# Preparing attention outputs one head earlier, and taking three quarters of the first merge products of four blocks into the last two heads

## The chip, the cores and the metric

One core of a Trainium2 chip runs one program: one layer of a hybrid bidirectional encoder. The metric is device time in microseconds (us) of that program; a change is measured against the kernel before on the same chip. On this core, TensorE (PE) multiplies matrices into PSUM, VectorE (DVE), ScalarE (ACT) and GpSimd (POOL) work elementwise, and SyncE (SP) issues most DMA transfers. Each engine takes its instructions in a fixed order.

## The reference, cut to what matters

The part of the layer that matters here is latent attention (MLA) with 16 heads over a prompt group of 256 tokens and a sample group of 1024 tokens, and what follows it:

```
s = (q_nope · k_nope + q_rope · k_rope) * scale
p = softmax(s);  o_a[head] = p @ v_a[head]                  # 16 heads of 64 columns
merged = sigmoid(gate_a) * (o_a @ p_a) + sigmoid(gate_b) * (o_b @ p_b)
x = x + gate * (merged @ w_out)
```

`o_b` is the output of the dilated attention; its half of `merged` has been computed earlier and lies in DRAM.

## The kernel before, in words

Tokens are 1280 columns in three chunks `CH`: two of 512 (sample) and one of 256 (prompt). Every float32 operand of a product is split into a high and a low part (`H`/`L`), so that each product of the reference is three matmuls: high by high, high by low, low by high.

**Heads** (loop at L1348 to L1365). A head has 17 steps: for two chunks eight key tiles each, then one step for the prompt group. A step computes scores (`scores`, L1172 to L1174, three matmuls into a PSUM tile `S`, three buffers), `soft` (L1126 and L1127 on ACT: the exponential twice, into `p` and `ph`; then `pl = p - ph` on POOL, L81, or on DVE for a chunk's first tile and the prompt), and a running sum of `p` on DVE (`ac`). The products with the values (`values`, L1210 and L1211) come three steps later (`LAG`). Beside each step, `fill` (L1334) advances two things: `tops`, which computes the row maxima of the head that comes next (`row_max`: a matmul L1107 into a PSUM tile `mi`, two buffers, and a DVE reduce L1108), and a side generator chosen by `others(h)` (L1313): projections of later heads, `row_sums` (L1147 to L1159: sums of `p` by PE, then through DRAM, reciprocals to `rz_d`). The side generator's pace is a number from `RATE` per step, against the cost that it yields. At the end of an even head, and of head 15, the rest of the side generator is run.

**Outputs.** Each pair of heads leaves its unnormalised output in DRAM (`oa_d`). `prep(k)` (L1251 to L1264) loads pair k's output and two halves of its reciprocals (three DMAs), multiplies them on DVE (`or<-or,or`), casts the high part on ACT (`x<-or`, L1263) and takes the low part on POOL (`x<-or,x`). In head 14 the side generator does this for pairs 0 to 5 in chunk 0, and then `row_sums(6)`; in head 15 it loads and splits weight block 0 of `p_a` (`pa_some`), prepares pair 6, and loads blocks 1 to 3. Pair 7 stays in SBUF and is prepared after the last head, behind the zb sums (L1372) that give its reciprocals. Heads 12 and 13 have no such work: head 13 has nothing in its side generator.

**Merge.** `merge(ms, c)` (L1420 to L1440) computes, for output blocks m of 128 columns, eight pairs by three matmuls into a PSUM tile `pe`; the first call takes blocks 0 to 3 of chunk 0 together: pairs 0 to 6 of each block, then pair 7 of each. Then, per block: `ga` and `mb` are loaded (256 KB each) into tiles `gm`, a sigmoid on ACT, `ga = ps * ga` on DVE, `ga += mb` on POOL, a cast to the high part on ACT (`R<-gm`, L1439), the low part on DVE. The `gm` tiles are a ring of four buffers. Blocks 4 to 7 follow one at a time (L1469 to L1476); ahead of each, `prep_r1` (L1452) prepares two pairs for chunks 1 and 2 together (tiles `R`, one load of 384 KB and two of 96 KB), and weight blocks 6, 7 and 0 are loaded. After that a loop (L1492 to L1497) goes over the eight blocks again for chunks 1 and 2, with weights loaded anew, and a `w_out` load for each.

The order of instructions on an engine is set when the program is built, by priorities and modelled times; all `mk` rings of buffers make a load wait until an earlier tile has been read for the last time.

Of the kernel before, what the change touches and what calls it, by code (L numbers as in the profile page):

```python
# [46 lines left out]
def kernel(  # L47
# [11 lines left out]
    def mk(pool, shape, dt=F32, tag=None, bufs=None):  # L59
        count[0] += 1  # L60
        kw = {}
        if bufs is not None:
            kw["bufs"] = bufs
        return pool.tile(shape, dt, name=f"{tag or 't'}_{count[0]}", tag=tag or f"u{count[0]}", **kw)

    def open_pool(name, side=None, space=None):
        kw = dict(space=space) if space is not None else dict(side=side)
        cm = tc.tile_pool(name=name, bufs=1, reuse_waits="tile", **kw)
        return cm, cm.__enter__()

    def close_pool(cm):
        cm[0].__exit__(None, None, None)
# [4 lines left out]
    def dve_tt(out, a, b, op):  # L77
        nc.vector.tensor_tensor(out=out, in0=a, in1=b, op=op)  # L78
# [50 lines left out]
    v_d = dram.tile([KD, P, NT, 2, 2, 64], F32R, name="v_d")  # L129
    m_d = dram.tile([NH, T], F32R, name="m_d")  # L130
    qr_d = dram.tile([2, 4 * P, T], F32R, name="qr_d")
    oa_d = dram.tile([KD, P, T], F32, name="oa_d")
    z_d = dram.tile([KD, 2, T], F32, name="z_d")
    rz_d = dram.tile([KD, 2, T], F32, name="rz_d")
# [892 lines left out]
    psM = open_pool("psM", space=PSUM)  # L1027
    okeep = {}
    LEAD = 5
    RATE = (3600, 700, 960, 960)  # L1030
    PB, LAG = (4, 5, 5), 3

    def mi():
# [235 lines left out]
    def x0(c=0):  # L1269
        return mk(opl, [P, 512], F32R, tag="x0", bufs=2 * KD)  # L1270

    def prep_some(ks):
        for k in ks:
            prep(k, (0,), or_tile, x0)
            yield 1000

    pa_w = {}

# [7 lines left out]

    oaH, oaL = [[None] * KD for _ in CH], [[None] * KD for _ in CH]
    def tail_pools():
        nonlocal opl, ocm, eacm
        close_pool(lcm)  # L1290
        close_pool(kcm)
        ocm = open_pool("oa", "right")
        opl = ocm[1]
        eacm = open_pool("ea", "right")
        okeep["o"] = mk(opl, [P, T], tag="o7", bufs=1)
        yield 0

    ocm = opl = eacm = None
# [11 lines left out]
    def projections(p_):  # L1310
        yield from ahead([job_p(p_, "k"), job_p(p_, "q")])

    def others(h):  # L1313
        p_ = h // 2
        if h == 0:
            return projections(1)
        if h % 2 == 0 and h < NH - 2:
            return chain(side[0], row_sums(p_ - 1))
        if h % 2 and p_ + 2 < KD:
            return projections(p_ + 2)  # L1320
        if h == NH - 2:
            return chain(tail_pools(), prep_some(range(KD - 2)), row_sums(p_ - 1))
        if h == NH - 1:
            return chain(pa_some((0,)), prep_some((KD - 2,)), pa_some((1, 2, 3)))
        return chain()

    def chain(*gens):
        for g in gens:
            yield from g
# [18 lines left out]
    for h in range(NH):  # L1348
        while h not in ready:
            next(tops)  # L1350
        now[0] = h
        while later:
            later.pop(0)()
        side = [others(h), 0.0, 0.0, (h > 0) + max(0, h - NH + 3)]
        hd = Head(h)
        for c, kt in [(c, kt) for c in range(2) for kt in range(NS)] + [(2, 0)]:
            pend.append((hd, c, kt, hd.step(c, kt)))
            fill()
            if (c, kt) == (0, LAG + 1) and h + 1 < NH:
                value_load(h + 1)  # L1360
            if len(pend) > LAG:
                p_ = pend.pop(0)
                p_[0].values(*p_[1:])
        if h % 2 == 0 or h == NH - 1:
            run(side[0])  # L1365
    for p_ in pend:
        p_[0].values(*p_[1:])
# [40 lines left out]
    epl = ecm[1]  # L1408
    psE = open_pool("psE", space=PSUM)

    def mm3_part(ps, w, x, ks, first, last):
        (wh, wl), (xh, xl) = w, x
        for k in ks:
            nc.tensor.matmul(ps, lhsT=wh[k], rhs=xh[k], start=first and k == ks[0], stop=False)
            nc.tensor.matmul(ps, lhsT=wh[k], rhs=xl[k], start=False, stop=False)
            nc.tensor.matmul(ps, lhsT=wl[k], rhs=xh[k], start=False, stop=last and k == ks[-1])

    mgH, mgL = [[chunk_set(0)] for _ in range(2)]

    def merge(ms_, c):  # L1420
        c0, n = CH[c]
        cs_ = slice(c0, c0 + n)
        pss = [mk(psE[1], [P, 512], tag="pe", bufs=8)[:, 0:n] for _ in ms_]
        x = (oaH[c], oaL[c])
        if len(ms_) > 1:
            for m, ps in zip(ms_, pss):
                mm3_part(ps, pa_w[m], x, range(KD - 1), True, False)
            for m, ps in zip(ms_, pss):
                mm3_part(ps, pa_w[m], x, range(KD - 1, KD), False, True)
        else:  # L1430
            mm3_part(pss[0], pa_w[ms_[0]], x, range(KD), True, True)
        for m, ps in zip(ms_, pss):
            ga, mb = [mk(epl, [P, 512], tag="gm", bufs=4)[:, 0:n] for _ in range(2)]
            nc.sync.dma_start(out=ga, in_=ga_d[m, :, cs_])
            nc.sync.dma_start(out=mb, in_=mb_d[m, :, cs_])
            nc.scalar.activation(out=ga, in_=ga, func=AF.Sigmoid)
            dve_tt(ga, ps, ga, ALU.mult)
            pool_tt(ga, ga, mb, ALU.add)
            nc.scalar.copy(out=mgH[c][m], in_=ga)  # L1439
            sub_dve(mgL[c][m], ga, mgH[c][m])  # L1440
# [530 lines left out]
```

## Time and profile before

| what | value |
|---|---|
| runs of the kernel before, us | 2473.57, 2468.44, 2470.86 (median 2470.86) |
| the profiled execution, us | 2468.41 |
| its span, us | 2466.6 (1.8 less than its time) |
| PE busy, share of the span | 95% |
| DVE, ACT, POOL busy | 61%, 44%, 45% |

All times in the trace are from the start of the span. In the page, PE's busy share dips below nine tenths in few slices; the stretch of this change is from 1260 to 1483 us. A PE that shows busy is not always at full speed: the granted clock (PEclk, 1.00 is 2.4 GHz, 0.50 is 1.2 GHz) falls after pauses.

### The profile page before, as it was taken

How to read it: one execution, taken by the hardware profiler on the slowest of the kernel's cores; microseconds unless marked ns; L12 is line 12 of the kernel's file. 1: busy time of each engine (PE TensorE's matmuls, PEld its weight loads, DVE VectorE, ACT ScalarE, POOL GpSimd, SP SyncE). 2: the span in 40 equal slices, each digit the busy share in tenths (PEclk: the TensorE clock that was granted, in tenths of full speed). 3: DMA queues.
4: the chain of work that ended last, by engine and by line, in shares of the span. 5: the costliest groups of instructions: out<-in, count | busy, mean ns of one | idle time of the engine just before them, and what ended most of it. 6: DMA issues, size and time to landing. Idle time of an engine off the chain costs nothing.

```text
span 2466.6 us, 36993 instructions
## 1 busy us (share of the span) xinstructions
PE 2355.0 (95%) x13177; PEld 1994.2 (81%) x13177; DVE 1502.2 (61%) x2467; ACT 1080.5 (44%) x2106; POOL 1109.5 (45%) x802
## 2 busy tenths in 40 slices
PE   7899999999999899999998999979999999999997
PEld 3789997666678777777776778769999999988876
DVE  4733332444446788888897533485655565568768
ACT  4431212554424477777776433353322332344434
POOL 1443331110125156666668441065565556539373
PEclk9999999999999999999999999989999999999999
DMA  7132225567467843333342763332232223177554
GB/s 262 47 130 93 100 85 177 180 193 247 142 171 251 280 119 83 82 82 85 87 111 85 216 185 115 124 112 86 85 110 88 82 81 110 64 249 242 171 182 165
DMA packets 274770, 342.87 MB, mean 139 GB/s; under 512 B 24397, under 2 KB 177758, under 8 KB 274586
## 3 DMA queue, kind: packets, MB, share of 16 engines
q1 hardware_dynamic: 248942, 311.40, 40.8%
q10 hardware_dynamic: 25644, 29.12, 3.4%
q8 instruction: 103, 1.69, 0.3%
q14 instruction: 81, 0.66, 0.1%
HBM read 237.06 MB, written 94.19 MB: 134 GB/s over the span
## 4 chain that ended last, share of the span: by engine, by line
PE 76%; DVE 8%; DMA 5%; issue 5%; POOL 4%; ACT 2%; SPq 1%; ACTq 0%; DVEq 0%; POOLq 0%
PE X L244 31%; PE Y L1796 7%; PE pp L100 7%; PE mi L1077 3%; PE mi L1107 2%; PE S L1173 2%; PE S L1172 2%; PE S L1174 2%; PE O L1211 2%; PE O L1210 2%; PE X L92 2%; PE X L94 2%; PE X L93 2%; POOL t L81 1%; PE X L467 1%
## 5 line engine op out<-in xcount | busy, mean ns | idle before, releaser
L244 PE MATMUL X<-t,wh 128*128 128x320 f32 x2864 | 540.1, 310 | 9.5 <-ACT wh L230 5.7
L244 PEld LDWEIGHTS X<-t,wh 128*128 128x128 f32 x2864 | 452.7, 189 | 10.3 <-ACT wh L230 5.9
L81 POOL TENSOR_TENSOR pl<-p,ph 128x512 fp32r<-128x512 f32 x224 | 298.1, 1340 | 135.6 <-ACT ph L1127 105.9
L244 PE MATMUL X<-t,wl 128*128 128x320 f32 x1432 | 328.0, 310 | 6.3 <-DVE wl L78 6.3
L244 PEld LDWEIGHTS X<-t,wl 128*128 128x128 f32 x1432 | 240.5, 189 | 7.2 <-DVE wl L78 6.7
L1126 ACT ACTIVATE p<-S 128x512 f32<-128x512 f32 x272 | 163.6, 601 | 105.4 <-issue 38.5
L100 PE MATMUL pp<-t,wh 128*128 128x512 f32 (+3 forms) x672 | 199.3, 376 | 0.6 <-DVE sm L598 0.5
L1108 DVE TENSOR_REDUCE m<-mi 128x1 f32<-128x512 f32 x256 | 174.0, 685 | 34.5 <-PE mi L1107 31.6
L81 POOL TENSOR_TENSOR wl<-wr,wh 128x512 fp32r<-128x512 f32 (+2 forms) x50 | 62.3, 1246 | 289.9 <-ACT wh L209 220.6
L230 ACT CAST wh<-wr 128x512 fp32r<-128x512 f32 x113 | 70.2, 621 | 273.2 <-PE X L244 175.7
L78 DVE TENSOR_TENSOR ut<-X,ut 128x640 f32<-128x640 f32 x126 | 101.5, 819 | 138.2 <-PE X L244 91.4
L81 POOL TENSOR_TENSOR wl<-R,wh 128x512 fp32r<-128x512 f32 x63 | 99.2, 1575 | 145.2 <-ACT wh L230 145.2
L1127 ACT ACTIVATE ph<-S 128x512 fp32r<-128x512 f32 x272 | 162.3, 597 | 1.3 <-issue 0.4
L1796 PE MATMUL Y<-bh,ah 128*128 128x512 f32 x385 | 152.1, 395 | 7.2 <-DVE ut L78 6.1
L1796 PE MATMUL Y<-bl,ah 128*128 128x512 f32 x385 | 152.1, 395 | 5.8 <-POOL bl L81 5.8
L1796 PE MATMUL Y<-bh,al 128*128 128x512 f32 x385 | 151.7, 394 | 0.0
L78 DVE TENSOR_TENSOR wl<-wr,wh 128x512 fp32r<-128x512 f32 x119 | 108.3, 910 | 55.8 <-ACT wh L230 49.0
L100 PEld LDWEIGHTS pp<-t,wh 128*128 128x128 f32 (+1 forms) x672 | 112.3, 185 | 32.8 <-issue 12.7
L244 PE MATMUL X<-R,wh 128*128 128x320 f32 x736 | 138.1, 309 | 0.0
L78 DVE TENSOR_TENSOR pt<-X,pt 128x640 f32<-128x640 f32 x60 | 48.6, 823 | 136.3 <-PE X L244 84.9
L78 DVE TENSOR_TENSOR al<-ar,ah 128x640 fp32r<-128x640 f32 x75 | 89.6, 1197 | 57.5 <-ACT ah L1770 51.9
L100 PE MATMUL pp<-t,wl 128*128 128x512 f32 (+3 forms) x336 | 122.2, 364 | 1.0 <-DVE wl L78 1.0
(431 smaller groups left out, 5709.4 us busy)
## 6 DMA issues: line engine op xcount, KB each, us to landing
ac_d<-ut SPq DMA_DIRECT2D x77, 320.0 KB
ar<-ac_d SPq DMA_DIRECT2D x75, 320.0 KB
R<-in_w_up_dram SPq DMA_DIRECT2D x84, 256.0 KB
br<-in_w_down_dram SPq DMA_DIRECT2D x77, 256.0 KB
ad<-in_ada_w_dram SPq DMA_DIRECT2D x64, 256.0 KB
wr<-in_w_in_dram SPq DMA_DIRECT2D x48, 256.0 KB
rw<-in_w_in_dram SPq DMA_DIRECT2D x20, 512.0 KB
V<-v_d SPq DMA_DIRECT2D x16, 640.0 KB
```

What stands on the lines that cost most here:

```text
L78: nc.vector.tensor_tensor(out=out, in0=a, in1=b, op=op)
L81: nc.gpsimd.tensor_tensor(out=out, in0=a, in1=b, op=op)
L92: nc.tensor.matmul(ps, lhsT=wh[k], rhs=xh[k], start=(k == 0), stop=False)
L93: nc.tensor.matmul(ps, lhsT=wh[k], rhs=xl[k], start=False, stop=False)
L100: nc.tensor.matmul(ps, lhsT=w[k], rhs=x[k], start=(k == 0 and w is wh and x is xh), stop=(k == n - 1 and w is wl))
L230: nc.scalar.copy(out=h, in_=a)
L244: nc.tensor.matmul(ps[:, z, 0:320], lhsT=a[:, k, :], rhs=b[q][k][:, 320 * z:320 * z + 320], start=(j == 0 and i == 0), stop=(j == n - 1 an ...
L1077: nc.tensor.matmul(ps[:, 0:n], lhsT=t[k], rhs=x[k][:, cs_], start=(k == 0 and t is wh and x is xh), stop=(k == kn - 1 and t is wl))
L1108: nc.vector.reduce_max(out=m2[:, i, c:c + 1], in_=ps, axis=AX.X)
L1126: nc.scalar.activation(out=p_, in_=ps, func=AF.Exp, scale=MSCALE)
L1127: nc.scalar.activation(out=ph, in_=ps, func=AF.Exp, scale=MSCALE)
L1796: nc.tensor.matmul(ps, lhsT=a[:, P * j:P * j + P], rhs=b, start=(f == 0 and a is ah and b is bh), stop=(f == HF - 1 and a is al))
```

## The change

Six preparations (pairs 0 to 5, chunk 0) go from head 14's side generator to head 13's, at a yielded cost of 1800 each. A new function `partial(m)` computes pairs 0 to 5 of block m (18 matmuls of 128x512) into an `mi` tile, copies it to SBUF on ACT, and stores it in DRAM (`pp_d`, 256 KB per block). Head 14 gets weight blocks 0 and 1, `row_sums(6)` and `partial(0)`; head 15 pair 6, `partial(1)`, block 2, `partial(2)`, block 3 and `partial(3)`. What head 14 has not done at its end goes on in head 15. The first merge then has only pairs 6 and 7 left for blocks 0 to 3 (24 matmuls, 96 before); for each of them the stored part is loaded into a third `gm` tile of the same ring of four, and added on DVE. `RATE` goes from 960 to 1100 for head 14 and to 2000 for head 15. `tail_pools` is split, since a pool that head 13 still reads can be closed only at head 14.

```diff
-    RATE = (3600, 700, 960, 960)
+    RATE = (3600, 700, 1100, 2000)
...
+    PARTS, KP = 4, KD - 2
+
+    def partial(m):
+
+        ps = mi()
+        for k in range(KP):
+            mm3_part(ps, pa_w[m], (oaH[0], oaL[0]), (k,), k == 0, k == KP - 1)
+            yield 3 * 512
+        t = ms()
+        nc.scalar.copy(out=t, in_=ps)
+        nc.sync.dma_start(out=pp_d[m], in_=t)
...
+        if h == NH - 3:
+            return chain(tail_pools(), prep_some(range(KP), 1800))
         if h == NH - 2:
-            return chain(tail_pools(), prep_some(range(KD - 2)), row_sums(p_ - 1))
+            return chain(side[0], tail_pools2(), pa_some((0, 1)), row_sums(p_ - 1), partial(0))
         if h == NH - 1:
-            return chain(pa_some((0,)), prep_some((KD - 2,)), pa_some((1, 2, 3)))
+            return chain(side[0], prep_some((KD - 2,)), partial(1), pa_some((2,)), partial(2), pa_some((3,)), partial(3))
...
-        if h % 2 == 0 or h == NH - 1:
+        if h % 2 == 0 and h != NH - 2 or h == NH - 1:
             run(side[0])
...
-                mm3_part(ps, pa_w[m], x, range(KD - 1), True, False)
+                mm3_part(ps, pa_w[m], x, range(KP, KD - 1), True, False)
...
+            if c == 0 and m < PARTS:
+                part = mk(epl, [P, 512], tag="gm", bufs=4)
+                nc.sync.dma_start(out=part, in_=pp_d[m])
+                dve_tt(part, ps, part, ALU.add)
+                ps = part
             dve_tt(ga, ps, ga, ALU.mult)
```

POOL in head 13 (`x` is the low part of a preparation, `pl` that of a step). Before, five instructions in the middle of the head:

```order
L81 TENSOR_TENSOR pl_13496<-p_13494,ph_13495 128x512
L81 TENSOR_TENSOR pl_13513<-p_13511,ph_13512 128x512
L81 TENSOR_TENSOR pl_13531<-p_13529,ph_13530 128x512
L81 TENSOR_TENSOR pl_13547<-p_13545,ph_13546 128x512
L81 TENSOR_TENSOR pl_13563<-p_13561,ph_13562 128x512
```

and now:

```order
L81 TENSOR_TENSOR x_3178_13457<-or_13450,x_3177_13456 128x512
L81 TENSOR_TENSOR pl_13522<-p_13520,ph_13521 128x512
L81 TENSOR_TENSOR pl_13539<-p_13537,ph_13538 128x512
L81 TENSOR_TENSOR x_3194_13504<-or_13497,x_3193_13503 128x512
L81 TENSOR_TENSOR pl_13557<-p_13555,ph_13556 128x512
L81 TENSOR_TENSOR pl_13583<-p_13581,ph_13582 128x512
```

Six `x` stand among head 13's `pl`, one behind every second or third.

PE in head 15, a step near the middle of the head (`S` scores, `O` values). Before:

```order
L1210 MATMUL O_14339<-ph_14304,V_13887 128x512
L1211 MATMUL O_14339<-pl_14305,V_13887 128x512
L1172 MATMUL S_14355<-qH_13266,kH_13061 128x512
L1173 MATMUL S_14355<-qH_13266,kL_13062 128x512
L1174 MATMUL S_14355<-qL_13267,kH_13061 128x512
```

and now:

```order
L1211 MATMUL O_14247<-ph_14319,V_13948 128x512
L1212 MATMUL O_14247<-pl_14320,V_13948 128x512
L1173 MATMUL S_14399<-qH_13267,kH_13062 128x512
L1174 MATMUL S_14399<-qH_13267,kL_13063 128x512
L1175 MATMUL S_14399<-qL_13268,kH_13062 128x512
L1293 MATMUL mi_14391<-x_3193_13503,e_3468_14381 128x512
L1294 MATMUL mi_14391<-x_3194_13504,e_3468_14381 128x512
L1295 MATMUL mi_14391<-x_3193_13503,e_3469_14382 128x512
```

A step of head 15 has eight matmuls where it had five; all 72 of the partial products stand ahead of head 15's last scores.

SP's queue from the merge's first load (`gm<-ga_d`, `gm<-mb_d` gates and the other half; `R` the outputs of a pair for chunks 1 and 2; `or` block 7 of `p_a`). Before:

```order
L1434 DMA gm_14625<-ga_d 128x512
L1435 DMA gm_14626<-mb_d 128x512
L1434 DMA gm_14634<-ga_d 128x512
L1435 DMA gm_14635<-mb_d 128x512
L1256 DMA R_3539_14661<-oa_d 128x768
...
L1256 DMA R_3564_14747<-oa_d 128x768
L1247 DMA R_3565_14748<-rz_d 64x768 x2
L206 DMA or_14761<-in_p_a_dram 128x4x128
L206 DMA or_14767<-in_p_a_dram 128x4x128
```

and now:

```order
L1458 DMA gm_14659<-pp_d 128x512
L1453 DMA gm_14666<-ga_d 128x512
L1257 DMA R_3557_14704<-oa_d 128x768
...
L1458 DMA gm_14683<-pp_d 128x512
L1453 DMA gm_14753<-ga_d 128x512
L1257 DMA R_3576_14776<-oa_d 128x768
L1248 DMA R_3577_14777<-rz_d 64x768 x2
L1454 DMA gm_14754<-mb_d 128x512
L207 DMA or_14790<-in_p_a_dram 128x4x128
L207 DMA or_14796<-in_p_a_dram 128x4x128
```

Before, four pairs' `R` loads and block 7 stood behind four `gm` loads; now block 7 stands behind fourteen, the last of them block 4's `mb`.

## Rows read from the trace of the kernel before

**Rows 1.** Stretches: length; busy PE, PEld, DVE, ACT, POOL; clock; DMA share; GB/s
```profile
1260.36:1284.51 24.15, 24.15 (x110) 19.24 (x108) 23.44 (x39) 19.62 (x40) 19.94 (x17) 1.00 0.32 86
1284.51:1320.48 35.97, 29.20 (x119) 19.75 (x118) 33.55 (x47) 23.32 (x47) 27.97 (x22) 0.95 0.35 105
1320.48:1347.89 27.41, 23.35 (x91) 16.77 (x90) 19.10 (x24) 21.81 (x44) 24.84 (x19) 0.94 0.32 88
1347.89:1360.39 12.50, 10.94 (x68) 9.06 (x66) 5.69 (x10) 3.52 (x8) 4.15 (x4) 0.80 0.07 22
1360.39:1382.90 22.51, 22.51 (x97) 18.55 (x96) 12.76 (x17) 10.60 (x20) 10.06 (x9) 0.96 0.89 234
1382.90:1405.24 22.34, 22.34 (x97) 18.06 (x96) 12.26 (x17) 8.94 (x16) 11.26 (x10) 1.00 0.76 222
1405.24:1440.00 34.76, 27.26 (x138) 21.94 (x137) 15.56 (x22) 15.56 (x30) 17.74 (x15) 0.95 0.74 221
```

**Rows 2.** PE's waits, 1284 to 1348: total us, times, longest
```profile
PE O L1211 <- POOL pl L81: 3.2, 4, 1.0
PE O L1210 <- issue: 2.5, 1, 2.5
```

**Rows 3.** Groups of head 14: busy us, mean ns, idle before
```profile
L81 POOL TENSOR_TENSOR x<-or,x 128x512 fp32r<-128x512 f32 x6 | 8.2, 1364 | 6.3 <-ACT x L1263 6.3
L78 DVE TENSOR_TENSOR or<-or,or 128x512 f32<-128x512 f32 x6 | 6.4, 1070 | 1.7 <-DMA or<-rz_d 1.7
L78 DVE TENSOR_TENSOR pl<-p,ph 128x512 fp32r<-128x512 f32 x3 | 4.2, 1404 | 0.3 <-ACT ph L1127 0.3
```

**Rows 4.** Groups of head 13
```profile
L1108 DVE TENSOR_REDUCE m<-mi 128x1 f32<-128x512 f32 x15 | 10.2, 678 | 0.1
L78 DVE TENSOR_TENSOR pl<-p,ph 128x512 fp32r<-128x512 f32 x3 | 2.3, 776 | 0.4 <-ACT ph L1127 0.3
```

**Rows 5.** PE's timeline in the merge: start us, us, instruction, wait before it
```profile
1365.00 0.39 PE L1415 MATMUL pe<-x,wh 128*128 128x512 f32 x1
1365.22 0.39 PE L1416 MATMUL pe<-x,wl 128*128 128x512 f32 x1
...
1408.75 0.50 PE L1414 MATMUL pe<-e,wh 128*128 128x512 f32 x1 [1.08 <-ACT e L1263]
...
1420.48 0.50 PE L1414 MATMUL pe<-e,wh 128*128 128x512 f32 x1 [1.86 <-ACT wh L209]
...
1432.59 0.50 PE L1414 MATMUL pe<-e,wh 128*128 128x512 f32 x1 [3.04 <-ACT wh L209]
...
1434.97 0.63 PE L1414 MATMUL pe<-e,wh 128*128 128x512 f32 x1
1435.40 0.63 PE L1415 MATMUL pe<-e,wh 128*128 128x512 f32 x1
```

**Rows 6.** SP's timeline in the merge: issue of loads
```profile
1373.81 1.13 SPq L206 DMA_DIRECT2D or<-in_p_a_dram  x2
...
1383.84 0.34 SPq L1434 DMA_DIRECT2D gm<-ga_d  x1
```

**Rows 7.** ACT's timeline in the merge
```profile
1379.42 0.62 ACT L209 CAST wh<-or 128x512 fp32r<-128x512 f32 x1 [1.87 <-DMA or<-in_p_a_dram]
...
1386.69 0.64 ACT L1436 ACTIVATE gm<-gm 128x512 f32<-128x512 f32 x1 [0.97 <-DMA gm<-ga_d]
```

**Rows 8.** Groups of the merge, 1360.39 to 1440
```profile
L81 POOL TENSOR_TENSOR gm<-gm,gm 128x512 f32<-128x512 f32 x11 | 15.5, 1413 | 9.8 <-DVE gm L78 6.0 <-DMA gm<-mb_d 1.6 <-issue 1.3
L78 DVE TENSOR_TENSOR gm<-pe,gm 128x512 f32<-128x512 f32 x11 | 7.5, 683 | 3.0 <-PE pe L1416 2.9
L1439 ACT CAST R<-gm 128x512 fp32r<-128x512 f32 x10 | 6.2, 619 | 14.5 <-POOL gm L81 14.5
L78 DVE TENSOR_TENSOR R<-R,R 128x768 f32<-128x768 f32 x7 | 6.7, 956 | 9.0 <-DMA R<-rz_d 9.0
L78 DVE TENSOR_TENSOR e<-R,e 128x512 fp32r<-128x512 f32 x7 | 5.2, 739 | 2.4 <-ACT e L1263 2.2
```

More of the change, by code (lines that the diff above doesn't have):

```diff
@@ L131 @@
     qr_d = dram.tile([2, 4 * P, T], F32R, name="qr_d")
+    pp_d = dram.tile([4, P, 512], F32, name="pp_d")
     oa_d = dram.tile([KD, P, T], F32, name="oa_d")
@@ L1270, in x0, with prep_some, mm3_part @@
         return mk(opl, [P, 512], F32R, tag="x0", bufs=2 * KD)
-    def prep_some(ks):
+    def prep_some(ks, cost=1000):
         for k in ks:
             prep(k, (0,), or_tile, x0)
-            yield 1000
+            yield cost
+    PARTS, KP = 4, KD - 2
[7 more added lines that the diff above has]
+        nc.sync.dma_start(out=pp_d[m], in_=t)
+    def mm3_part(ps, w, x, ks, first, last):
+        (wh, wl), (xh, xl) = w, x
+        for k in ks:
+            nc.tensor.matmul(ps, lhsT=wh[k], rhs=xh[k], start=first and k == ks[0], stop=False)
+            nc.tensor.matmul(ps, lhsT=wh[k], rhs=xl[k], start=False, stop=False)
+            nc.tensor.matmul(ps, lhsT=wl[k], rhs=xh[k], start=False, stop=last and k == ks[-1])
     pa_w = {}
@@ L1288, in tail_pools, with tail_pools2 @@
     def tail_pools():
-        nonlocal opl, ocm, eacm
+        nonlocal opl, ocm
         close_pool(lcm)
-        close_pool(kcm)
         ocm = open_pool("oa", "right")
         opl = ocm[1]
+        okeep["o"] = mk(opl, [P, T], tag="o7", bufs=1)
+        yield 0
+    def tail_pools2():
+        nonlocal eacm
+        close_pool(kcm)
         eacm = open_pool("ea", "right")
-        okeep["o"] = mk(opl, [P, T], tag="o7", bufs=1)
         yield 0
@@ L1409 @@
     psE = open_pool("psE", space=PSUM)
[L1411 to L1416, printed above, removed]
     mgH, mgL = [[chunk_set(0)] for _ in range(2)]
```

## The prediction

> **What bounds the kernel now.** I read the stretches first. Head 13 is full: PE 24.15 us busy of 24.15 at clock 1.00, DVE 23.44, POOL 19.94. Head 14, with the six preparations in it, takes 35.97 with PE 29.20 busy and DVE 33.55; head 15 takes 27.41 with POOL 24.84 and PE 23.35, at clock 0.94; from its last scores to the merge there are 12.50 more. PE fills the merge of chunk 0 (22.51 and 22.34), then has 27.26 of 34.76 [rows 1]. So heads 14 and 15 are held by the elementwise engines, and hold room for PE work; the merge of chunk 0 is held by PE; what follows is held by loads and splits. PE's waits in heads 14 and 15 name them: 3.2 us for POOL's `pl`, 2.5 in one pause [rows 2]. Behind the merge of chunk 0 PE waits 1.08, 1.86 and 3.04, and after the last of these the next products come 0.43 apart (1434.97, 1435.40) where they are else 0.22 apart (1365.00, 1365.22) [rows 5]: a pause over some 3 us costs about 2 us more at the lower of the two clock levels. I take 0.23 us for a product of 128x512.
>
> **The change, part by part.**
>
> *Head 13* gets six preparations. Each is a POOL low part of 1.364 and a DVE product of 1.070 as they ran in head 14 [rows 3]. POOL: 19.94 + 8.2 = 28.1. DVE: 23.44 + 6.4, less three reduces of 0.678 [rows 4] that the new order puts behind head 13's last scores, = 27.8. PE loses their three products: 23.4. So POOL and DVE, nearly level, are the bound; head 13 now has its fullest engine beside PE, DVE, at 97% of its length, so I take 28.1 / 0.97 = 29.0: **+4.9**. Ends: -0.7 if PE still sets it; +7.3 if DVE and POOL slow each other as in head 14, where DVE's `pl` takes 1.404, against 0.776 in head 13 [rows 3, 4].
>
> *Head 14* loses the preparations. PE at full speed: head 13's 24.15, about 0.7 for row sums in place of some row maxima, 0.7 for the three products that come over, 18 × 0.23 = 4.1 for block 0's part: 29.7. DVE: 33.55 - 6.4 + 2.0 = 29.2. Since head 14's maxima end later, its first `qL` is likely late; 0.8 for that gives 30.5: **-5.5**. Ends: -6.3 with no wait, -3.0 with a pause like the 2.5 [rows 2].
>
> *Head 15*: 24.15 less the row maxima, about 3.9, is 20.2; with 54 × 0.23 = 12.4 it is 32.6, and POOL's 24.84 hides in it. I take 32.8: **+5.4** (ends +5.2 and +6.6). The parts' ACT copies (0.6 each by the casts [rows 8]) and 1 MB of stores lie beside a DMA that is a third busy [rows 1]. *To the merge*: POOL is no longer behind at the end of head 15, and of the 1.56 us that PE idles in the 12.50 I take **-1** (ends -1.5 and 0).
>
> Heads together: +4.9 - 5.5 + 5.4 - 1 = **+3.8** (ends -3.3 and +10.9).
>
> *The merge* loses 72 × 0.23 = 16.6 us of PE work. What is late next decides what is kept. Let M be its first product, 1360.39 before. A block now takes three `gm` tiles of a ring of four, and by the program's waits the next block's stored part is loaded only when POOL's sum of the block before has freed a tile. One turn of that ring: a load, 2.85 from 1383.84 to the sigmoid at 1386.69 [rows 6, 7]; the added DVE sum, not in the trace of before, as its neighbour from PSUM, 0.68; the product 0.68; POOL's sum 1.41 [rows 8]: 5.6. Between the two DVE instructions stands a low part of another pair, 0.74 [rows 8]; with the crossings I take 6.5. The first block ends at M + 7.8 (15 products, part of them slow, 5; then 2.8), the fourth at M + 27.3. SP's loads of block 7 and of half the `R` tiles stand behind, in order. Block 7's are issued at M + 26.3, before at 1373.81, M + 13.4 [rows 6]; its cast, before 5.6 later (1379.42 [rows 7]) and now behind the casts of blocks 3 and 4, is at M + 31.5. PE has 96 products till it needs it, M + 23.6: a new wait of 8, and 2 for the clock. It ends block 7 at M + 40 (before M + 44.9) and meets the next late thing, pair 3's high part in chunk 1. On DVE and ACT there stand, behind block 3's low part (M + 28.6), three pairs' products, casts and low parts (0.96, 0.62, 0.74), blocks 5 and 6 with their POOL sums (3.4 each), three weight or block low parts (0.68), and pair 3's own product and cast (1.6) [rows 8]: about 17.4, with crossings M + 47. Before, this was the wait that ended at 1408.75, M + 48.4 [rows 5]. So the two kernels are nearly level there: 1.4 earlier, 2 given back to the clock. Behind it the 1.86 falls away, for ACT now casts the second half of block 1's weights ahead of the third `w_out` tile, and 1.2 of the 3.04. In sum **-2.5**: 14 of 16.6 given back.
>
> Ends: with a turn of 5.6 each date moves 2.7 earlier, and with the later waits filled ahead -9; with a load of 5.6 in the turn instead of 2.85 (as block 7's took [rows 6, 7]) +5.7.
>
> Sum: 3.8 - 2.5 = **+1.3** us. The profiled execution's 2468.41 becomes 2469.7; it lies 2.45 below the median of the runs, 2470.86, which becomes **2472**. I count a difference under 0.2% (4.9 us) as none, about what a measurement of this kernel can tell from it.
>
> **A rule that speaks against it.** DVE's `pl` with two SBUF operands takes 1.404 in head 14, beside POOL's preparations, and 0.776 in head 13; its reduces from PSUM take 0.678 in head 13 with POOL 83% busy [rows 1, 3, 4]. So it is the instructions with two SBUF operands that lose. The Trainium skill (SBUF — State Buffer, "SBUF: two separate sides") says that such a DVE instruction and a GpSimd one share a port pair under an exclusive lock: the other fully blocks. By that rule nothing of the six products would run beside POOL, and the sum would be that of the port rival below, 2478, instead of 2472. The rows agree with the sign; whether nothing overlaps they leave open, and I give this a rival of its own.
>
> **The rivals.** *The ring holds SP's queue (slower).* A turn costs 9.2 because its load lands in 5.6; block 7 and pair 3 come 8 us later, the merge is +5.7, all +9.5: **2480**. For it: SP's order, and the 5.6. Against: fewer loads are then under way at once than when 5.6 was seen (234 GB/s, 0.89 [rows 1]). It decides from a turn of 7.7 on. *The port (slower).* Head 13 is POOL's 28.1 plus six products of 0.68 and three `pl` of 0.776 one after the other, 34.5: +10.4 in place of +4.9, in all +6.8: **2478**. For it: rows 3; against: that head's POOL and DVE are 27.97 and 33.55 busy in 35.97 [rows 1]. *The ring turns at its floor (faster).* 5.6 per turn, -9 in the merge, and head 13 nearer to its engines' mean, heads +1.5: -7.5, **2463**. For it: the dates above add every crossing; against: DVE's order. *All products are saved (faster)*: -16.6 + 3.8 = -12.8, **2458**, if block 7 and pair 3 come in time; against: SP's order. That the products do not move is out: their order shows them in heads 14 and 15.
>
> **How the numbers follow.** Forecast 0.42; ring slower 0.22, port 0.08: slower 0.30. Ring at its floor 0.20, all saved 0.08: faster 0.28. The range, 2460 to 2481, leaves out the last rival (0.08), and of the two rivals by the ring what lies beyond their own prices; it takes in most of the heads' ends. The forecast's own range is 2466 to 2476.
>
> **What would show it.** In the new profile: head 13 near 29 with POOL near 28 busy; head 14 near 30.5 and head 15 near 33 with PE full and clock 1.00; in the merge a PE wait for block 7's `wh` of some 8 us, SP idle between the `gm` loads of blocks 1 to 3 at turns of 6.5, and pair 3's high part near M + 47. Head 13 under 26, or no wait at block 7, would make it wrong to the fast side; turns over 7.7 or head 13 over 33 to the slow side.

## The result and the profile after

| | kernel before | changed kernel |
|---|---|---|
| median of five runs each, us | 2471.21 | 2482.35 |
| lowest and highest of the changed kernel, us | | 2479.76 to 2486.21 |
| span of the profiled execution, us | 2466.6 | 2480.2 |

The ratio is 1.0051, with a 95% interval of 1.004 to 1.0063: slower by 11 us, where the forecast was +1.3 and the range ended at 2481. The stretches of the changed kernel, cut as in [rows 1] (length; busy PE, PEld, DVE, ACT, POOL; clock; DMA share; GB/s): heads 13, 14, 15, to the merge, then the first 22.51, the next 22.34 and 34.76 us of the merge.

```profile
1256.23:1285.65 29.42, 25.40 (x105) 17.96 (x104) 28.86 (x38) 21.25 (x42) 25.55 (x20) 1.00 0.48 133
1285.65:1324.46 38.81, 34.56 (x141) 24.17 (x140) 31.46 (x50) 24.64 (x50) 27.45 (x22) 0.91 0.35 101
1324.46:1357.05 32.59, 32.59 (x146) 26.48 (x144) 15.59 (x22) 21.57 (x42) 21.68 (x17) 1.00 0.11 37
1357.05:1372.24 15.19, 12.49 (x68) 11.23 (x66) 5.59 (x11) 4.37 (x9) 3.08 (x4) 0.65 0.11 36
1372.24:1394.75 22.51, 22.51 (x93) 18.17 (x92) 14.13 (x18) 9.40 (x17) 10.01 (x8) 0.93 0.72 210
1394.75:1417.09 22.34, 10.53 (x34) 7.28 (x32) 14.21 (x17) 8.84 (x17) 9.37 (x9) 0.69 0.98 266
1417.09:1451.85 34.76, 29.96 (x151) 25.49 (x152) 18.20 (x23) 15.33 (x30) 19.46 (x16) 0.90 0.80 230
```

Term by term, from these two executions:

| stretch | before | after | change | forecast |
|---|---|---|---|---|
| head 13 | 24.15 | 29.42 | +5.3 | +4.9 |
| head 14 | 35.97 | 38.81 | **+2.8** | **-5.5** |
| head 15 | 27.41 | 32.59 | +5.2 | +5.4 |
| to the merge | 12.50 | 15.19 | +2.7 | -1 |
| merge, first to last product | 122.19 | 121.17 | -1.0 | -2.5 |
| sum | 222.22 | 237.18 | +15.0 | +1.3 |

Heads 13 and 15 and the merge came out near their terms. Head 14 is 8.3 us off; the stretch to the merge is 3.7 off. Outside these five stretches the two executions differ by 1.4 us the other way.

**Head 14.** Its first 20 us and the rest:

```profile
1285.65:1305.65 20.00, 16.84 (x66) 10.33 (x65) 15.41 (x26) 9.41 (x19) 11.17 (x9) 0.83 0.33 93
1305.65:1324.46 18.81, 17.72 (x77) 13.84 (x76) 16.05 (x25) 15.24 (x32) 16.28 (x13) 1.00 0.37 111
```

PE started 66 matmuls in the first 20.00 us and 77 in the following 18.81. Head 15, which is full, runs 146 in 32.59, 0.223 us apart. At that distance the 66 are 14.7 us of work and the 77 are 17.2. So 5.3 of the lost time lie in the first 20 us: PE is idle for 3.2 of them, and the rest is a lower granted clock (0.83). Over the whole head PE is idle for 4.25 us and busy 3.1 us longer than its 141 matmuls would take at head 15's distance (31.5). The kernel before, with the preparations still in head 14, has as many matmuls in the first 20 us of that head:

```profile
1284.51:1304.51 20.00, 16.68 (x66) 12.38 (x65) 19.08 (x25) 13.62 (x27) 16.02 (x13) 0.91 0.42 122
```

So with most of the preparations gone DVE is less busy there (15.41 after 19.08) and POOL too (11.17 after 16.02), and PE gets no further. What stands there in the changed kernel, first POOL's timeline (start, us, instruction, wait before it):

```profile
1283.54 4.21 POOL L81 TENSOR_TENSOR pl<-p,ph 128x512 fp32r<-128x512 f32 x3
1287.71 1.30 POOL L81 TENSOR_TENSOR x<-or,x 128x512 fp32r<-128x512 f32 x1
1288.96 1.73 POOL L81 TENSOR_TENSOR e<-wr,e 128x512 fp32r<-128x512 f32 x1
1290.66 1.26 POOL L81 TENSOR_TENSOR pl<-p,ph 128x512 fp32r<-128x512 f32 x1
```

then PE's, SP's and ACT's:

```profile
1291.97 0.50 PE L1212 MATMUL O<-pl,V 128*128 128x512 f32 x1 [2.43 <-POOL pl L81]
```

```profile
1290.72 0.39 SPq L207 DMA_DIRECT2D wr<-in_p_a_dram  x1
1291.70 0.29 SPq L1121 DMA_DIRECT2D qL<-m_d  x1
1295.50 0.56 SPq L1048 DMA_DIRECT2D V<-v_d  x1
```

```profile
1295.98 0.60 ACT L1127 ACTIVATE p<-S 128x512 f32<-128x512 f32 x1 [5.26 <-PE S L1175]
1304.40 0.36 ACT L1137 COPY ms<-O 64x256 f32<-64x256 f32 x1 [2.36 <-DMA oa_d<-ms]
```

A preparation's low part (`x`) and a weight block's (`e`) stand on POOL ahead of the `pl` that PE needs, and PE pauses 2.43. Behind that pause the granted clock is 0.53 from 1293.00 to 1300.30, near the lower of its two levels. SP's load of the next weight tile (`wr`) goes out as POOL's `e` ends, at 1290.69, and behind it in SP's order `qL` and `V`; ACT then waits 5.26 for the scores, and later 2.36 for an earlier store of `ms`. The load of head 14's `qL` is issued 6.05 us after the start of the stretch, 1285.65. (All stretches start at the scores of the prompt step, the last of the head before.) In the kernel before it was issued 0.11 after the start. Head 12 of the kernel before, an undisturbed even head with 140 matmuls, has `qL` 3.9 ahead of its start, 1230.89, a full PE, and a POOL 60% busy; its SP line, its first 20 us and its whole stretch:

```profile
1226.98 0.24 SPq L1120 DMA_DIRECT2D qL<-m_d  x1
```

```profile
1230.89:1250.89 20.00, 19.96 (x98) 15.37 (x96) 17.73 (x29) 14.03 (x27) 11.53 (x10) 1.00 0.53 127
1230.89:1260.36 29.47, 29.43 (x140) 22.30 (x139) 24.71 (x42) 20.92 (x42) 17.81 (x14) 1.00 0.52 125
```

**The merge.** With M, the time of the merge's first product, at 1372.24, PE's timeline shows the wait for block 7 that the prediction named, and pair 3 in chunk 1:

```profile
1407.02 0.80 PE L1293 MATMUL pe<-x,wh 128*128 128x512 f32 x1 [10.80 <-ACT wh L210]
1408.74 0.80 PE L1295 MATMUL pe<-x,wl 128*128 128x512 f32 x1 [0.50 <-POOL wl L81]
...
1424.08 0.80 PE L1293 MATMUL pe<-e,wh 128*128 128x512 f32 x1 [3.77 <-ACT e L1264]
```

SP's timeline has the ring's turns (the `gm` load of each next stored part) and block 7's load, here at 1400.70:

```profile
1380.24 0.33 SPq L1458 DMA_DIRECT2D gm<-pp_d  x1
...
1388.27 0.33 SPq L1458 DMA_DIRECT2D gm<-pp_d  x1
...
1395.18 0.33 SPq L1458 DMA_DIRECT2D gm<-pp_d  x1
...
1400.70 0.98 SPq L207 DMA_DIRECT2D or<-in_p_a_dram  x2
```

The first of these loads was issued at 1372.99, so the turns are 7.2, 8.0 and 6.9 us; block 7 is issued at M + 28.5, and pair 3 comes at M + 51.8.

### The profile page after: what moved, and what is told of

It reads as the page before. It is cut to its first block, busy times and chain, and to the rows that moved or that the text cites. A ratio compares the mean times of both kernels' runs of the same rounds, so it can differ in the third digit from the quotient of the medians.

```text
span 2480.2 us, 37010 instructions
## 1 busy us (share of the span) xinstructions
PE 2358.7 (95%) x13177; PEld 1996.8 (81%) x13177; DVE 1508.9 (61%) x2471; ACT 1083.5 (44%) x2110; POOL 1110.4 (45%) x802
## 4 chain that ended last, share of the span: by engine, by line
PE 76%; DVE 8%; DMA 5%; issue 4%; POOL 4%; ACT 2%; SPq 1%; ACTq 0%; DVEq 0%; POOLq 0%
PE X L245 31%; PE Y L1820 7%; PE pp L100 6%; PE mi L1078 3%; PE mi L1108 2%; PE S L1174 2%; PE S L1173 2%; PE S L1175 2%; PE O L1212 2%; PE O L1211 2%; PE X L92 2%; PE X L94 2%; PE X L93 2%; POOL t L81 1%; DVE t L78 1%
## 5 line engine op out<-in xcount | busy, mean ns | idle before, releaser
L81 POOL TENSOR_TENSOR wl<-wr,wh 128x512 fp32r<-128x512 f32 (+2 forms) x50 | 61.4, 1228 | 288.1 <-ACT wh L210 219.5
```

What stands on the lines that cost most here:

```text
L81: nc.gpsimd.tensor_tensor(out=out, in0=a, in1=b, op=op)
```

## The experiments

All ratios are to the kernel before, run on the same chip. "Heads" is the time from the start of head 13's stretch to the merge's first product, and "merge" the time from there to the last product, both from one profiled execution each. The kernel before has 100.0 and 122.2, the changed kernel 116.0 and 121.2.

| run | head 13 | head 14 | head 15 | to merge | heads | merge | ratio |
|---|---|---|---|---|---|---|---|
| before, a second execution | 24.13 | 37.15 | 25.88 | 12.49 | 99.7 | 124.2 | |
| preparations alone | 29.44 | 37.90 | 23.78 | 14.44 | 105.6 | 125.6 | 1.0026 |
| parts alone | 24.13 | 37.45 | 35.89 | 12.96 | 110.4 | 122.4 | 1.0016 |
| parts alone, other ring | 24.02 | 39.28 | 35.89 | 12.15 | 111.3 | 121.7 | 1.0021 |
| change, other ring | 29.44 | 38.62 | 32.61 | 12.50 | 113.2 | 120.9 | 1.0039 |
| three preparations, no parts | 27.53 | 33.83 | 26.74 | 13.56 | 101.7 | 125.3 | 0.9994 |
| change, no part loads | 29.43 | 38.61 | 32.55 | 15.28 | 115.9 | 122.4 | 1.0043 |
| change, maxima ahead | 32.33 | 37.91 | 32.28 | 14.24 | 116.8 | 122.2 | 1.0058 |
| change, low parts on DVE | 29.44 | 40.02 | 33.02 | 14.41 | 116.9 | 124.1 | 1.0049 |
| change, both of these | 32.45 | 37.33 | 32.27 | 13.63 | 115.7 | 120.9 | 1.0039 |
| change, merge loads first | 29.44 | 38.64 | 32.58 | 15.36 | 116.0 | 116.9 | 1.0026 |
| three preparations, parts, merge loads first | 25.07 | 38.06 | 33.53 | 15.12 | 111.8 | 117.2 | 1.0019 |
| before, merge loads first | 24.13 | 39.12 | 25.67 | 14.93 | 103.9 | 123.9 | 0.9994 |

### The two halves of the change, each alone

The preparations alone: moved to head 13, no parts, the first merge and the paces as before.

```diff
-    RATE = (3600, 700, 1100, 2000)
+    RATE = (3600, 700, 960, 960)
...
-            return chain(side[0], tail_pools2(), pa_some((0, 1)), row_sums(p_ - 1), partial(0))
+            return chain(side[0], tail_pools2(), row_sums(p_ - 1))
...
-                mm3_part(ps, pa_w[m], x, range(KP, KD - 1), True, False)
+                mm3_part(ps, pa_w[m], x, range(KD - 1), True, False)
```

> Only the six preparations move to head 13; no partial products, merge as before. Packed preparations (theory 1: they overload DVE and POOL in head 13, and the backlog breaks the start of head 14): head 13 near 29.4 us, head 14 still with the pause of some 2.4 us near its start and the lower clock behind it, near 34 (38.8 less 18 products of 0.23), so slower than before by 3 to 6 us. Partial products (theory 2: head 14's 8 us beyond the plan come from the partial products and weight blocks put into it): head 13 near 29.4, head 14 near 27 to 29, no slower than before.

Measured: ratio 1.0026 (1.0014 to 1.0038), slower. Head 14 took 37.90 us without one product of a part and without the preparations that had filled it. Its first 20 us (stretches, columns as above):

```profile
1288.51:1308.51 20.00, 16.61 (x56) 9.38 (x54) 13.93 (x23) 9.84 (x19) 12.01 (x10) 0.70 0.29 86
```

So head 14 is nearly as long without the parts as with them (38.81, and theory 1 had 34 here), and it did not get shorter than before when the preparations left it.

The parts alone: the preparations stay in head 14, the four parts go to head 15.

```diff
-    RATE = (3600, 700, 1100, 2000)
+    RATE = (3600, 700, 960, 2500)
...
-        if h == NH - 3:
-            return chain(tail_pools(), prep_some(range(KP), 1800))
...
+            return chain(tail_pools(), tail_pools2(), prep_some(range(KP)), row_sums(p_ - 1))
...
+            return chain(side[0], pa_some((0,)), prep_some((KD - 2,)), partial(0), pa_some((1,)), partial(1), pa_some((2,)), partial(2), pa_some((3,)), partial(3))
```

> Preparations stay in head 14 as before; all four blocks' partial products in head 15 (72 products there). Theory 1: heads 13 and 14 as before (24.2 and 36.0), head 15 near 20.2 + 16.6 = 37, the first merge product some 10 us later than before, and with the ring as in the change the merge returns 1 to 3: slower than before by 7 to 9, faster than the change by 3 to 6. Theory 2: no better than the change.

Measured: 1.0016 (1.0006 to 1.0026). Head 15 pays 8.5 us of the 16.6 us of products, and the merge gives back next to nothing (122.4, beside 122.2 and 124.2 in two executions of the kernel before). So either half alone is slower, the preparations by the heads, the parts because the merge does not get shorter by what leaves it.

### The ring of `gm` tiles

The stored part's tile comes from the `or` ring in place of the `gm` ring, in the change and in the parts alone.

```diff
-                part = mk(epl, [P, 512], tag="gm", bufs=4)
+                part = mk(opl, [P, 512], tag="or", bufs=4)
```

> The change, with the stored parts loaded into the four idle weight staging tiles instead of the gate tiles, so that a block takes two of the ring of four again. Theory 3 (the ring holds SP's queue, and through it block 7 and pair 3): a turn falls from 6.5 to 8 us to 3.5 to 5, PE's wait for block 7 from 10.8 to under 5, pair 3 of chunk 1 comes 4 to 8 us earlier; total 4 to 8 us under the change. Rival (the transfers themselves are the limit, 266 GB/s at a DMA share of 0.98 in the stretch after the first merge): the wait only changes its place, total within 2 us of the change. Heads 13 to 15 as in the change either way.

> Both edits: preparations as before in head 14, partial products in head 15, stored parts in the weight staging tiles. Theories 1 and 3 together: heads as in the run with partial products only (+10 against before), the merge some 8 to 10 faster than before: within 3 us of before. If the transfers are the limit: 7 to 9 slower than before.

Measured: 1.0039 (1.0024 to 1.0054) and 1.0021 (1.0009 to 1.0032). PE's timeline of the first of them, in which M = 1377.20:

```profile
1398.66 0.51 PE L1293 MATMUL pe<-x,R 128*128 128x512 f32 x1 [1.95 <-ACT R L210]
...
1410.80 0.79 PE L1293 MATMUL pe<-x,wh 128*128 128x512 f32 x1 [3.96 <-ACT wh L210]
...
1428.88 0.80 PE L1293 MATMUL pe<-e,wh 128*128 128x512 f32 x1 [3.77 <-ACT e L1264]
```

Block 7's wait falls from 10.80 to 3.96, another of 1.95 appears ahead of it, and pair 3 comes at M + 51.7 as before; the merge takes 120.9. The ring sets one date and not the merge. Theory 3 is not borne out: the ratios with and without the edit, 1.0039 and 1.0051, are 3 us apart with overlapping intervals, and 1.0021 is 5 us, between the two forecasts of the other run.

### The loads of the parts

The four loads and DVE sums of the stored parts are left out, so that the output lacks pairs 0 to 5 of blocks 0 to 3 in chunk 0. All else stays.

```diff
-            if c == 0 and m < PARTS:
+            if False:
```

> The change without the four loads of the stored parts and without adding them (the output lacks pairs 0 to 5 of four blocks in chunk 0); 1 MB less to move, and two gate tiles per block. If the transfers set the merge: block 7 and pair 3 come 3 to 5 us earlier than in the change, the merge with all its products falls from 121 to 116 to 118, total 3 to 5 us under the change. If the order of SP's queue or the chain on DVE and ACT sets it, not the bytes: within 2 us of the run with its own staging tiles, 121.

Measured: 1.0043 (1.0028 to 1.0058). Pair 3 comes at M + 45.6, six us earlier, and the merge takes 122.4 all the same. PE's waits in it (total us, times, longest):

```profile
PE pe L1293 <- ACT wh L210: 9.8, 4, 4.2
PE pe L1293 <- ACT e L1264: 3.6, 1, 3.6
```

In the changed kernel the first of these lines is 12.1 in two waits. Block 7 accounts for 3.85 here, and the longest wait now stands at M + 87.4, for a later weight block: what is saved ahead is waited for behind.

### The kernel before, profiled a second time

> The kernel before, profiled a second time, to see how far the local stretches move between executions. If they repeat: head 13 24.2, head 14 36.0, head 15 27.4, to the merge 12.5, the merge with all its products 122.2, each within 0.5 us. If the pauses in head 14 and the clock vary from one execution to the next: head 14 between 36 and 39, the stretch to the merge between 12 and 15.

Measured: 2469.37 us beside 2470.79 in that comparison. Head 14 took 37.15 and the merge 124.2, against 35.97 and 122.2. A single execution fixes these stretches to a few us, no better. Three other runs leave heads 13 and 14 as the kernel before has them (the parts alone with either ring, and the kernel before with the merge's loads first); their head 14 took 37.45, 39.28 and 39.12.

### Half of the preparations

As the preparations alone, with pairs 0 to 2 in head 13 and 3 to 5 in head 14.

```diff
-            return chain(tail_pools(), prep_some(range(KP), 1800))
+            return chain(tail_pools(), prep_some(range(3), 3600))
...
+            return chain(side[0], tail_pools2(), prep_some(range(3, KP)), row_sums(p_ - 1))
```

> Three of the six preparations in head 13, three in head 14; no partial products, merge as before. Theory 1 with a threshold (head 13 has room for some preparations, not for six): head 13 near 26.5, head 14 33 or less, head 15 26 or less; a few us faster than before. If the start of head 14 breaks for another reason than the number of preparations (the late row maxima): head 14 still 37 or more, and slower than before by 2 to 5.

Measured: 0.9994 (0.9983 to 1.0005), the same as before and not the few us faster of theory 1. Head 14 took 33.83, the shortest of all. Its first 20 us had 73 matmuls:

```profile
1283.76:1303.76 20.00, 19.05 (x73) 11.41 (x71) 17.13 (x27) 12.52 (x25) 15.45 (x13) 0.83 0.39 113
```

Heads 13 and 14 together: 60.1 to 63.3 in the five executions that have them as before, 61.4 with three preparations moved, 67.3 with six. The first three cost nothing that these executions can tell, the other three some six us; the ratios, 0.9994 and 1.0026, differ by 0.0032, or 8 us, with the merges alike (125.3 and 125.6).

### Which engine holds head 14's start

Four row maxima of head 14 are taken ahead of head 13's first step, so that `qL` is early:

```diff
+        if h == NH - 3:
+            for _ in range(4):
+                next(tops, None)
```

> The change, with row maxima four steps ahead from head 13 on, so that head 14's largest values reach it before its first scores. If the late maxima (the row of qL that the third score product of head 14's first step waits for) break the start of head 14: head 13 near 31 (four reduces of 0.68 more), head 14 near 31 to 33 instead of 38.8, heads together 4 to 6 us shorter, total 3 to 6 us under the change. If POOL's and DVE's backlog from the preparations breaks it: head 14 still 36 or more, total within 2 us of the change or above.

Measured: 1.0058 (1.0041 to 1.0074). `qL` was issued 3.14 us ahead of head 14's stretch, and head 14 took 37.91: PE now waited 2.0 for POOL's `pl`, and POOL was busy 15.87 of the first 20. Head 13 grew by 2.9, by four more reduces on the engine that bounds it, and head 14 lost 0.9 with 6 matmuls fewer. The late `qL` alone is not the cause.

Four low parts go from POOL to DVE:

```diff
-            (sub_dve if k0 else sub_pool)(lo[:, 0:n, :], raw[:, 0:n, :], h[:, 0:n, :])
+            (sub_dve if k0 or dve else sub_pool)(lo[:, 0:n, :], raw[:, 0:n, :], h[:, 0:n, :])
...
-            (sub_dve if c == 1 or k == KD - 1 else sub_pool)(lo, s, h)
+            (sub_dve if c == 1 or k == KD - 1 or c == 0 and k in (4, 5) else sub_pool)(lo, s, h)
...
+        pa_w[m] = load_w(wpl, p_a[:, P * m:P * m + P], P, 4, WB, raw_of=raw_of, of=of, dve=m in (0, 1) and m not in pa_w)
```

> The change, with four low parts taken from POOL to DVE: those of pairs 4 and 5 and the first half of weight blocks 0 and 1 in the heads. In the changed kernel POOL entered head 14 with about 4 us of such work ahead of the first `pl`, PE paused 2.4 us for that `pl`, the weight block's second load waited for POOL in SP's queue with qL, V and the stores behind it, and the next 12.6 us ran at clock 0.73. Theory 1 (POOL's backlog breaks head 14's start): the pause is under 1 us, the clock of head 14 is 0.98 or more, and head 14 takes 31 to 34 instead of 38.8; head 13 gains 0 to 1.5 since DVE is its bound; total 4 to 7 us below the changed kernel. Theory 2 (partial products or late row maxima hold head 14): head 14 stays at 37 to 39, and PE's pause stays with another name. Theory 3 (SP's queue alone): the pause of PE goes but the bubble near the third step stays, head 14 35 to 37.

Measured: 1.0049 (1.0031 to 1.0068). POOL is idle 7.62 us early in head 14, and the head takes 40.02. PE's waits in it name DVE ahead of POOL:

```profile
PE mi L1108 <- DVE m L1109: 2.4, 5, 0.7
PE O L1212 <- POOL pl L81: 1.6, 2, 1.1
```

POOL's queue was the wait that one saw, not what had to be removed. My expectation of 31 to 34 fell.

Both edits together:

> The change with both relieved at once: four row maxima of head 14 ahead of head 13's first step (so that DVE enters head 14 with fewer reduces and qL is loaded early), and the four low parts on DVE instead of POOL. Each alone left head 14 at 37.9 and 40.0: with the maxima ahead, PE still paused 2.0 for POOL's `pl`; with the low parts on DVE, PE's row maxima came 1.2 us apart behind a full DVE and qL was issued 5.0 after head 14's first scores. Theory 1 (the work that the packed preparations push over the boundary, on whichever of DVE and POOL is fuller, starves PE): with both relieved head 14 takes 31 to 35 at clock 0.97 or more, qL is issued before head 14's first scores, PE's longest wait is under 1.2; head 13 takes 32 to 34, so that the two together are no more than 1 to 3 us below the changed kernel's 68.2. Theory 4 (the partial products and the row sums themselves hold head 14): 37 or more again.

Measured: 1.0039 (1.0023 to 1.0055), head 14 37.33 where 31 to 35 was expected. No wait of PE's is above 0.7 now, and DVE is full in the first 20 us; the rest is full with PE:

```profile
1288.22:1308.22 20.00, 17.55 (x66) 9.76 (x64) 19.19 (x28) 10.60 (x19) 9.24 (x7) 0.91 0.32 86
1308.22:1325.55 17.33, 16.51 (x72) 12.61 (x70) 13.34 (x22) 15.09 (x31) 13.72 (x11) 1.00 0.28 82
```

Theory 1 of that run fell in its size, and 37.33 is what theory 4 (the parts and the row sums hold head 14) forecast. Against the parts stands the run without them, with 37.90; the row sums stand in every version of head 14, and no run tested them. What the three runs show is that the loss changes its place: without POOL's low parts DVE is the wait, and with the maxima taken ahead head 13, which DVE bounds, grows by more than head 14 loses. A plain lack of time on DVE or POOL is not shown: in the changed kernel DVE is busy for 15.41 and POOL for 11.17 of the head's first 20 us.

### The order of the merge's loads

Pairs 0, 4, 1, 5 of chunks 1 and 2 and weight blocks 6 and 7 are put ahead of the sums of blocks 0 to 3, in the change, in the change with three preparations in head 14, and in the kernel before.

```diff
+        if between:
+            between()
...
+    def first():
+        for k in (0, 4):
+            prep_r1(k)
+        pa_load(6, None, r1_w)
+        for k in (1, 5):
+            prep_r1(k)
+        pa_load(7, lambda: mk(opl, [P, 4, P], tag="or", bufs=4))
...
+    merge((0, 1, 2, 3), 0, first)
```

> The change, with pairs 0, 4, 1, 5 of chunks 1 and 2 and weight blocks 6 and 7 put ahead of the sums of blocks 0 to 3, so that SP issues their loads ahead of the first gm load; heads untouched (116 us, as in the changed kernel). Theory A (place in SP's queue behind the ring's turns sets block 7 and pair 3): block 7's wait of 10.8 falls under 3, pair 3 comes before M+46, and the merge takes 108 to 115 instead of 121: total 6 to 12 us below the changed kernel. Theory B (loads and splits of the whole stretch set the end, whatever their order): another wait takes its place, the merge stays at 119 to 125, total within 3 us of the changed kernel.

> As the run before, with pairs 0 to 2 prepared in head 13 and 3 to 5 in head 14 ahead of block 0's part. Theory 1 and A: head 13 27.5, head 14 34 to 36, head 15 with the rest of the parts 33 to 36, to the merge 12.5 to 13.5: heads 107 to 112 instead of 116, merge 108 to 115, total 0.994 to 0.999 of the kernel before. Theory B: heads the same, merge 119 to 125, total 1.001 to 1.004. If the parts, and not the packed preparations, slow head 14, head 14 is 38 or more here as well.

> The kernel before, with nothing but the order of the merge's second preparations: pairs 0, 4, 1, 5 of chunks 1 and 2 and weight blocks 6 and 7 ahead of the sums of blocks 0 to 3. Heads as before (about 100). Theory A (order in SP's queue decides part of the merge's end, with or without the parts): the waits behind chunk 0 (1.1, 1.9 and 3.0 us in the kernel before) shrink to under 2 together, the merge takes 113 to 119 instead of 122 to 124, ratio 0.995 to 0.999. Theory B (transfers and splits as a whole): the merge stays at 121 to 125 and the ratio within 0.002 of 1.

Measured: 1.0026 (1.0012 to 1.004), 1.0019 (1.0006 to 1.0031) and 0.9994 (0.9981 to 1.0006). PE's waits of the first, in which M = 1374.13:

```profile
1406.82 0.50 PE L1293 MATMUL pe<-e,wh 128*128 128x512 f32 x1 [3.38 <-ACT wh L210]
...
1415.99 0.50 PE L1293 MATMUL pe<-e,wh 128*128 128x512 f32 x1 [2.33 <-ACT e L1264]
...
1458.91 0.79 PE L1293 MATMUL pe<-e,wh 128*128 128x512 f32 x1 [4.04 <-ACT wh L210]
```

Block 7's wait is gone and pair 3 comes at M + 41.9, as theory A had it. The waits are now for the weights of chunk 1 (`pe<-e`), the first at its first block and the longest at M + 84.8. The merge falls to 116.9 and 117.2 with the parts, 4 us, and not to the 108 to 115 of theory A; without the parts it stays at 123.9, theory B. So the order of loads is worth some 4 of the 16.6 us that the parts take out of the merge; the ratio, 1.0026 after 1.0051, is 6 us lower, the low end of what theory A had for the total. The second run has heads of 111.8 with head 14 at 38.06, where its expectation had named 38 or more as the mark of parts that slow the head. That is 4.2 more than with three preparations and no part, and the part's 18 products are 4.0 at 0.223 each: by these two executions head 14 pays for its part in full. They carry this only roughly, for head 13, edited alike in both, took 25.07 and 27.53. DVE is nearly full there again (18.67 of the first 20.00 us). No version tried is faster than the kernel before.

## Why the prediction was wrong

**Head 14, "-5.5": the step that failed.** The prediction took it that with the preparations gone the head is as long as its fullest engine is busy, PE with 29.7, and allowed 0.8 for a late `qL`. Of the 8.3 us that it missed, 1.8 are PE's own work: 141 matmuls are 31.5 at head 15's distance. The other 6.5 are pauses of PE and the lower clock behind them, 7.3 us where the term had 0.8. Three things were wrong in it.

First, the two sums were low. DVE had 31.46 us in 50 instructions where 29.2 was forecast: one product of the six preparations slid over the boundary and that of pair 6 came in, with two more running sums of `p` and one more low part of a weight block. The three more reduces came as counted.

Second, and more: the larger of two sums is a forecast for work that overlaps. In the first 20 us of head 14 PE gets 56 to 73 matmuls in all the versions run, the kernel before among them, where head 12 gets 98. The part's products come at 1304.11 and later, 12 of the 18 in the stretch in which PE is nearly full anyway.

Third, the prediction took from [rows 1] that head 14 was long for its preparations. Taken out, they left 37.90. What it could have seen in the trace of before is that heads 1 to 12 take 29.4 to 30.7 each, PE full in those I looked at (head 12, above), and that the pause of 2.5 in [rows 2] ends at 1296.54, in those first 20 us, with no engine named for it.

Shown by the runs: the parts are not needed for the loss (37.90 without them), nor does it go with the late `qL` alone (37.91) or with POOL's low parts alone (40.02); moving three preparations in place of six avoids it (33.83, without parts). What the common cause is stays open. My reading is elementwise work that piles up at the boundary; for it stands that six preparations cost and three do not. Against it stands that neither DVE nor POOL is full at the start of head 14 in the changed kernel. No run took that work away without adding it elsewhere, and none tested the row sums, so it is argued, not shown.

**To the merge, "-1".** Measured +2.7. PE idled 2.70 us there where it had idled 1.56, since its wait for DVE's `ms` rose from 0.7 to 2.5; the prediction had it fall. And the matmul of one column (L1398, 40 of them) took 6.9 us in all where the same group took 4.9 before, at a granted clock of 0.65 against 0.80 [rows 1]. The clock is not the change's doing alone: with the same order the run with the other ring had 12.50 at 0.81, and the kernel before with another merge order 14.93 at 0.66. The run with the other ring has the longer wait as well. What decides the clock stays open. The term should have had ends of -1.5 and +3.

**Head 13, "+4.9"** came out as +5.3, with DVE at 28.86 of 29.42 where I had put it at 97% of the length and POOL at 28.1. The total was right by two errors that cancel. Fewer of the six ran inside the head, five products and four low parts, and each product took longer (groups of head 13):

```profile
L1109 DVE TENSOR_REDUCE m<-mi 128x1 f32<-128x512 f32 x13 | 8.8, 675 | 0.0
L78 DVE TENSOR_TENSOR or<-or,or 128x512 f32<-128x512 f32 x5 | 8.5, 1704 | 0.0
L81 POOL TENSOR_TENSOR x<-or,x 128x512 fp32r<-128x512 f32 x4 | 5.1, 1285 | 1.3 <-ACT x L1264 1.3
L78 DVE TENSOR_TENSOR pl<-p,ph 128x512 fp32r<-128x512 f32 x3 | 3.1, 1026 | 0.3 <-ACT ph L1128 0.3
L78 DVE TENSOR_TENSOR ac<-p,p 128x512 f32<-128x512 f32 x2 | 1.9, 930 | 0.0
L78 DVE TENSOR_TENSOR ac<-ac,p 128x512 f32<-128x512 f32 x8 | 5.5, 693 | 0.1
```

The product is 1704 where [rows 3] had 1070; the reduce from PSUM, 675, has not moved from [rows 4]. The port rival, +10.4 in this head, was wrong in size and right in kind. The Trainium skill (SBUF — State Buffer, "SBUF: two separate sides") has a DVE instruction with two SBUF inputs and a GpSimd one that reads SBUF exclude each other, for the whole of the one that started first. The trace bears that out. DVE's and POOL's timelines have the longest product and the `pl` beside it:

```profile
1272.17 3.06 DVE L78 TENSOR_TENSOR or<-or,or 128x512 f32<-128x512 f32 x1
```

```profile
1270.91 3.78 POOL L81 TENSOR_TENSOR pl<-p,ph 128x512 fp32r<-128x512 f32 x3
```

POOL's third `pl` ends at 1274.69, the product 0.54 later. Three more of the five products end 0.5 to 0.6 after a POOL instruction under way, and the fifth, which began at 1266.62 as a POOL instruction ended, took 0.68. The running sums tell the two kinds apart: `ac<-p,p` has two SBUF operands and took 930 on average, where it took 691 in head 13 before; `ac<-ac,p`, whose `ac` is a PSUM tile (L1194), kept 693. The head is not the 34.5 of that rival since five products and four low parts ran in it, and POOL had pauses that DVE could use.

**Head 15, "+5.4"** was +5.2: PE 32.59 of 32.59 at clock 1.00, POOL's 21.68 hidden.

**The merge, "-2.5"** was -1.0 against one execution of the kernel before and -3.0 against the other. Its main statement, that 14 of the 16.6 us go back to block 7 and pair 3, held. The sizes were off by a few us: turns of 7.2, 8.0 and 6.9 for 6.5, block 7's load at M + 28.5 for 26.3, its wait 10.8 for 8, pair 3 at M + 51.8 for 47. Behind block 7's wait 11 products took 5.2 us, a second pause of 0.50 left out, where they take 2.5 at full clock: 2.7 for the 2 that was put on the clock. One sum had a slip: a load at M + 26.3 and 5.6 to its cast make M + 31.9, not 31.5. The cause given, the ring in SP's queue, was too narrow. Another ring and no part loads shortened the wait at block 7 to 3.96 and 3.85, another order of loads removed it, and the merge came to 120.9, 122.4 and 116.9, since waits for later weight blocks took its place. What bounds those, beyond the order of the loads, was not settled.

**The rivals.** The ring rival's number, 2480, was nearest, but by another way: with the ring's hold loosened the change was still slower, 1.0039. That the products would all be saved (2458) and the ring at its floor (2463) are both refuted.

## What to carry to other kernels

A stretch takes the maximum of its engines' sums only if their work is spread alike over it: head 14's first 20 us had 66 matmuls before and after most of the preparations left them. Before moving elementwise work from one stage into the stage before, look at the boundary between them: which engine enters the next stage with a queue, and what the first wait there is for. And products that are taken out of a stage held by loads and splits are worth what the next wait leaves over: of 16.6 us some 0 to 3 here, and 5 to 7 with another order of loads, while head 15 alone grew by 8.5 in the run with nothing but the parts.

## What was not expected of the hardware

A DVE product of two SBUF operands, 128x512, took 1.70 us on average in a head in which POOL was 87% busy, and 0.68 in the one of them that ran in head 14's first 20 us in the run with both edits, where POOL was 46% busy; reduces from PSUM kept 0.675 in the first of these heads and 0.68 in the other. Most of the difference is waiting for POOL's instruction to end.

The same heads in the same order came out differently from one execution to the next where clock and waits meet: 35.97, 37.15 and 39.12 us for head 14 as the kernel before has it (clock 0.95 in the first, 0.83 in the last), and 12.5 to 15.4 for the last stretch before the merge. With the six preparations moved, four executions of head 14 gave 38.6 to 38.8.
